# Loading the first token tiles and weights at once, sharing the first squares between two engines, and filling TensorE's first waits with throwaway matmuls

## The chip, the cores and the metric

The kernel runs on all 8 cores of one Trainium2 chip: two dies, cores 0 to 3 and cores 4 to 7. The metric is the device time of the slowest core, in microseconds (us). Every timed run also lists the span and the mean granted TensorE clock of each core. Some runs are in a slow state: one die, or two of its cores, at a lower mean granted clock and behind the others (a run of e5 took 2133 us with die 0 at 0.812 to 0.813 and die 1 at 0.992 to 0.993; one of e1 took 1826 us with cores 6 and 7 at 0.976 to 0.977 and the others at 0.992 to 0.994). They are left out of every comparison here. Three groups of experiments were timed, one on a chip called 2 here and two on a chip called 6; within a group all kernels share the runs of the kernel before.

## The reference, cut to what matters

One step of a decoder layer: a half-step feed-forward block, a mixer (windowed attention, a recurrence, cross attention), a second half-step feed-forward block. Each core takes one prompt of 2048 tokens and 4 sample tokens. Only the start of the first feed-forward block matters here:

```python
D_MODEL = 1024
D_FF = ((8 * D_MODEL // 3 + 127) // 128) * 128   # 2816
EPS = 1e-6

def rmsnorm(x, g):
    xf = x.astype(jnp.float32)
    y = xf * lax.rsqrt(jnp.mean(xf * xf, axis=-1, keepdims=True) + EPS)
    return (y * g.astype(jnp.float32)).astype(x.dtype)

def half_ffn(x, g, w_gate, w_up, w_down):
    h = rmsnorm(x, g)
    return (jax.nn.silu(h @ w_gate) * (h @ w_up)) @ w_down
# ... in reference():
    xp = xp + 0.5 * half_ffn(xp, *ffn1)
# ... mixer, merge, second half_ffn, final rmsnorm
```

## The kernel before

The tokens of a core form six tiles of 336 to 352 tokens. A tile of x lies in SBUF as 128 partitions (features) times 8 chunks of its n tokens, in f32. The head of the kernel is the time until TensorE runs without gaps: tiles 0, 1 and 2 must be loaded, normalised and written as bf16 to `hT` before the gate and up matmuls of the first half can use them. A weight tile (`wp`, from `wgu`) feeds 2 x 8 matmuls for each of the three x tiles, 48 in all.

```python
    def sq(k, c, late=1000.0, pair=True):            # square of chunk c of tile k, summed by TensorE
        n = FT[k][1]
        if c == 0:
            pss[k] = P.tile(psS)
        p = pss[k]
        b = P.tile(brp)
        if not pair:
            actf(b.t[:, 0:n], xv(k, c), AF.Square, [dx[k][c]], [b.d])          # ScalarE
            mm(p.t[:, 0:n], ones_n, b.t[:, 0:n], c == 0, c == 7, [b.d, dc], [p.d], late=late)
        # ... other form, used later

    def lnexp(out, in_, power, reads, writes):       # (mean square + eps) ** power
        actf(out, in_, AF.Ln, list(reads) + [dc], writes, bias=epsc)
        actf(out, out, AF.Exp, writes, writes, scale=power)

    def to_h(k, r, g):                               # VectorE: x * gain * rstd -> hT
        t0, n = FT[k]
        for c in range(8):
            stt(DVE, hT[:, c, t0:t0 + n], xv(k, c), g[:, c:c + 1], r.t[:, 0:n], ALU.mult, ALU.mult, [dx[k][c], r.d, dc], [dh[k][c]])

    def load_x(k, src, parts=1, after=(), queues=(SP,)):
        n = FT[k][1]
        w = 8 // parts
        for q in range(parts):
            dst, sr = xv(k, q * w, w), src[k][:, q * w * n:(q + 1) * w * n]
            P.dma(queues[q % len(queues)], lambda e, dst=dst, sr=sr: e.dma_start(out=dst, in_=sr), reads=list(after), writes=dx[k][q * w:(q + 1) * w])

    def gate_up(half, w, hook=None):
        for j in range(NJ):
            b = load_w(w[j].rearrange("p a c n -> p (a c n)"), 2048, first_w[min(j, 5)] if hook else ())
            wv = b.t[:, :].rearrange("p (a c n) -> p a c n", a=2, c=8)
            for k in HT[half]:
                # ... 8 gate and 8 up matmuls into PSUM, Silu on ScalarE, product on VectorE
            if hook:
                hook(j)

    first_w = [dx[0][0:4], dx[0], dx[1][0:4], dx[1], dx[2][0:4], dx[2]]
# ... the start:
    load_x(0, xt, 4, queues=(SP, ACT))
    # ... constants; vecs (gains) loaded on the ACT queue, behind x
    for k in range(3):
        if k:
            load_x(k, xt, 2, after=dx[k - 1][0:5] if k == 1 else dx[k - 1][0:4])
        for c in range(8):
            sq(k, c, 0.0, False)
        to_h(k, rstd(k), gf1)
```

First, loads are gated: the second tile of x waits for the first, and the j-th weight tile waits for the part of x named in `first_w`. Second, the program is recorded, and a list scheduler in the file decides each engine's order of instructions once, before the run, from believed durations and believed landing times (`DMA_RATE`). On the chip each engine then works in that order, whatever really lands first (the trace below has ScalarE idle for 6.44 us before a square whose data is missing, with an Exp that is ready behind it).

The softmax here doesn't subtract the row's maximum and nothing guards it: scores larger than these inputs give would overflow.

Of the kernel before, what the change touches and what calls it, by code (L numbers as in the profile page):

```python
# [9 lines left out]
ALU = mybir.AluOpType  # L10
# [164 lines left out]
class Prog:  # L175
# [5 lines left out]
    TABLE = 1300.0  # L181
    SWISSUE = 800.0
    WAIT = 1200.0

    def __init__(self, nc, lanes=None):
        self.nc = nc
# [56 lines left out]
    def schedule(self):  # L243
# [61 lines left out]
        while done < n:  # L305
# [76 lines left out]
            if e == ACT and o["aset"] not in (None, table):  # L382
                cost += self.TABLE
                table = o["aset"]
            o["t0"] = start
            if o["dma"]:
                issue = self.SWISSUE if e == POOL else 60.0
                end = free[e] = start + issue
                if o["pool"] == "bulk":
                    fin = start + 12000.0  # L390
                else:
                    pipe[e] = max(pipe[e], start + issue) + o["nbytes"] / self.DMA_RATE[e]
                    fin = pipe[e] + self.DMA_FIX
            else:
                end = free[e] = start + cost
                fin = end + (self.PEDRAIN if e == PE else 0.0)
# [30 lines left out]
    def emit(self):  # L427
        nc = self.nc
        order = self.schedule()
        seq = []  # L430
        pos = {e: 0 for e in COMPUTE}
        for o in sorted(self.all, key=lambda o: o["t0"]):
            e = o["eng"]
            seq.append(order[e][pos[e]])
            pos[e] += 1
        streams, rr = {}, {}
        for o in seq:
            s = o["eng"]
            if o["dma"]:
                q = o["pool"]  # L440
                k = rr.get(q, 0)
                rr[q] = k + 1
                s = ("dma", q, k % self.lanes[q])
            lst = streams.setdefault(s, [])
            o["stream"], o["idx"], o["sig"] = s, len(lst), o["dma"]
            lst.append(o)
        known = {e: {} for e in COMPUTE}
        for o in seq:
            e = o["eng"]
            kn = known[e]  # L450
            deps = {}
            for j in o["preds"]:
                p = self.all[j]
                s, k = p["stream"], p["idx"]
                if not (s == e == PE) and deps.get(s, -1) < k:
                    deps[s] = k
            if o["dma"] and o["idx"] > 0:
                s = o["stream"]
                deps[s] = max(deps.get(s, -1), o["idx"] - 1)
            waits = [(s, k) for s, k in sorted(deps.items(), key=lambda x: str(x[0])) if kn.get(s, -1) < k]  # L460
            o["waits"] = [(s, k) for s, k in waits
                          if not any((s2, k2) != (s, k) and streams[s2][k2]["know"].get(s, -1) >= k for s2, k2 in waits)]
            for s, k in waits:
                for s3, k3 in list(streams[s][k]["know"].items()) + [(s, k)]:
                    if kn.get(s3, -1) < k3:
                        kn[s3] = k3
            for s, k in o["waits"]:
                streams[s][k]["sig"] = True
            o["know"] = dict(kn)
        semval = {}  # L470
        for s, lst in streams.items():
            c, vals = 0, []
            for o in lst:
                if o["sig"]:
                    c += 16 if o["dma"] else 1
                vals.append(c)
            semval[s] = vals
        with ExitStack() as st:
            sems = {}
            for s in streams:  # L480
                if any(o["sig"] for o in streams[s]):
                    sems[s] = st.enter_context(nc.semaphore("s_" + (s if isinstance(s, str) else f"{s[1]}{s[2]}")))
            block = st.enter_context(nc.Block())

            def run(name):
                def body(e):
                    b = Bound(e)
                    for o in order[name]:
                        for s, k in o["waits"]:
                            e.wait_ge(sems[s], semval[s][k])  # L490
                        inst = o["fn"](b)
                        if o["sig"]:
                            inst.then_inc(sems[o["stream"]], 16 if o["dma"] else 1)
                return body
            block.tensor(run(PE))
            block.scalar(run(ACT))
            block.vector(run(DVE))
            block.gpsimd(run(POOL))
            block.sync(run(SP))
# [51 lines left out]
def build_nc():  # L551
    nc = bass.Bass("TRN2", target_bir_lowering=False)
    P = Prog(nc)
# [78 lines left out]
    psS = P.pool(bu[5:8], True, 0)  # L632
    psM = P.pool(bu[0:7], True, 14)
    psO = P.pool(bu[7:8], True, 0)

    ident_f, ones_f = cf[:, 0:128], cf[:, 128:256]
    ident_b, ones_b, ones_n, ones_h = (cb[:, k * 128:(k + 1) * 128] for k in range(4))
# [44 lines left out]
    def load_w(src, n, after=()):  # L682
        b = P.tile(wpool)
        dst = b.t[:, 0:n]
        P.dma(POOL, lambda e: e.dma_start(out=dst, in_=src), reads=list(after), writes=[b.d])
        return b
# [9 lines left out]
    def xv(k, c, m=1):  # L696

        t0, n = FT[k]
        o = 8 * (t0 - 1024 * (k // 3)) + c * n
        return (XA, XB)[k // 3][:, o:o + m * n]  # L700
# [4 lines left out]
    def sq(k, c, late=1000.0, pair=True):  # L705
# [12 lines left out]
        else:  # L718
# [2 lines left out]
            tt(POOL, b.t[:, 0:n], s.t[:, 0:n], s2.t[:, 0:n], ALU.add, [s.d, s2.d], [b.d])  # L721
            mm(p.t[:, 0:n], ones_n, b.t[:, 0:n], c == 1, c == 7, [b.d, dc], [p.d], late=late)

    def rstd(k):
        n = FT[k][1]
        r = P.tile(frp)
        p = pss[k]
        lnexp(r.t[:, 0:n], p.t[:, 0:n], -0.5, [p.d], [r.d])
        return r
# [13 lines left out]

    def gate_up(half, w, hook=None):
        for j in range(NJ):
            b = load_w(w[j].rearrange("p a c n -> p (a c n)"), 2048, first_w[min(j, 5)] if hook else ())
            wv = b.t[:, :].rearrange("p (a c n) -> p a c n", a=2, c=8)
            for k in HT[half]:
                t0, n = FT[k]
                pg, pu = P.tile(psA), P.tile(psA)  # L750
                for p, a in ((pg, 0), (pu, 1)):
                    for c in range(8):
                        mm(p.t[:, 0:n], wv[:, a, c, :], hT[:, c, t0:t0 + n], c == 0, c == 7, [b.d, dh[k][c]], [p.d])
                s = P.tile(frp)
                actf(s.t[:, 0:n], pg.t[:, 0:n], AF.Silu, [pg.d], [s.d])
                o = t0 - 1024 * half
                tt(DVE, act[:, j, o:o + n], pu.t[:, 0:n], s.t[:, 0:n], ALU.mult, [pu.d, s.d], [dact[half][k % 3]])
            if hook:
                hook(j)

    first_w = [dx[0][0:4], dx[0], dx[1][0:4], dx[1], dx[2][0:4], dx[2]]

    def down(half, w, done):
        def one(k, dp, bs):
# [594 lines left out]
        return 1760e3  # L1359


    load_x(0, xt, 4, queues=(SP, ACT))
    P.op(POOL, lambda e: e.memset(vec[:, 60:61], 1.0), writes=[d_one])
    P.op(ACT, lambda e: e.activation(out=vec[:, 63:64], in_=vec[:, 60:61], func=AF.Ln), reads=[d_one], writes=[d_one])
    P.op(DVE, lambda e: e.memset(ones_n, 1.0 / 1024), writes=[dc])
    P.op(DVE, lambda e: e.memset(vec[:, 61:62], EPS), writes=[dc])
    P.op(DVE, lambda e: e.memset(vec[:, 62:63], 0.0), writes=[dc])
    P.dma(ACT, lambda e: e.dma_start(out=vec[:, 0:52], in_=vecs), writes=[dc])
    for k in range(3):
        if k:  # L1370
            load_x(k, xt, 2, after=dx[k - 1][0:5] if k == 1 else dx[k - 1][0:4])
        for c in range(8):
            sq(k, c, 0.0, False)
        to_h(k, rstd(k), gf1)
    P.op(POOL, lambda e: e.memset(ones_b, 1.0), writes=[dm])
    P.op(POOL, lambda e: e.memset(ones_h, 1.0 / 128), writes=[dm])
    P.op(POOL, lambda e: e.memset(rst, 1.0), writes=[dm])
    P.op(POOL, lambda e: e.memset(cb[:, 896:1408:64], 0.0), writes=[dm])
    for q, (src_, dst_) in enumerate(bulk):
        dd = Dep()  # L1380
        P.dma(ACT, lambda e, src_=src_, dst_=dst_: e.dma_start(out=dst_, in_=src_), writes=[dd], pool="bulk", rel=bulk_at(q / nbulk))
# [1 line left out]
    def hook(j):  # L1383
        if j == 3:
            mem_load()
        elif j == 5:
            P.dma(ACT, lambda e: e.dma_start(out=cf[:, :], in_=cstf), reads=d_memT, writes=[dm])
            P.dma(POOL, lambda e: e.dma_start(out=cb[:, 0:128], in_=cstb[:, 0:128]), reads=d_memT, writes=[dm])
            P.dma(POOL, lambda e: e.dma_start(out=cb[:, 512:896], in_=cstb[:, 128:512]), writes=[dm])
        elif j == 6:  # L1390
            mem_norm()
        elif j in (7, 8):
            mem_k(j - 7)
        elif j == 9:
            mem_v()
        elif j in (10, 12, 14):
            k = 3 + (j - 10) // 2
            switch(dx[k], d_memT + d_mhT)
            load_x(k, xt)
        elif j in (16, 18, 20):  # L1400
            k = 3 + (j - 16) // 2
            for c in range(8):
                sq(k, c)
            to_h(k, rstd(k), gf1)
# [222 lines left out]
```

## Time and profile before

| | before |
|---|---|
| time, median of 3 runs | 1809.42 us (1807.29 to 1811.98) |
| spans of the cores in the profiled run | 1797.5 to 1802.6 us |
| core 2 (slowest), `hT` of tiles 0, 1, 2 begun | 22.3, 31.8, 42.9 us |
| core 2, 97th gate/up matmul (the third weight tile) begun | 53.5 us |

The profiled run is not itself one of the timed runs, so its spans are compared only with spans. A count is taken from the trace, in which a matmul may be missing now and then (the page below lists 12105 matmuls and 12171 weight loads).

The first part of the page of the kernel before (core 2) gives busy time, share of the span and number of instructions by engine:

```profile
PE 1738.2 (96%) x12105; PEld 1109.0 (62%) x12171; DVE 674.7 (37%) x1391; ACT 730.4 (41%) x1266; POOL 405.2 (22%) x543
```

TensorE (PE) is the limit, at 96%. What can be won lies where it isn't busy, and that is the head. Stretches of 10 us of core 2; the columns are from:to, length, busy us with instruction counts of each engine, the granted TensorE clock (1.00 is full), the DMA engines' busy share and GB/s:

```profile
core 2: us, PE busy (x) PEld busy (x) DVE busy (x) ACT busy (x) POOL busy (x), PEclk, DMA share, GB/s
20.00:30.00 10.00, 5.30 (x24) 2.77 (x24) 4.58 (x9) 7.35 (x12) 1.59 (x3) 1.00 0.99 263
30.00:40.00 10.00, 7.80 (x40) 4.47 (x40) 3.95 (x9) 6.95 (x14) 1.06 (x2) 0.83 1.04 196
40.00:50.00 10.00, 6.42 (x26) 3.48 (x27) 4.86 (x10) 5.94 (x12) 0.00 (x0) 0.66 0.64 143
```

In a full stretch later on, TensorE does about 70 matmuls in 10 us (73 from 80 to 90 us, at a granted clock of 1.00); here it does 24, 40 and 26, and part of them at a granted clock of 0.66 to 0.83. The timeline of core 2 shows the chain (start, duration, engine, operation, output and inputs, count; in brackets the idle time before it and what ended it). In these lines `XA` is x, `br` a square, `hb` the sum of squares in PSUM, `fr` what ScalarE writes (Ln, Exp or Silu), `ps` and `nd` the gate and up results in PSUM, `wp` a weight tile:

```profile
14.17 0.56 ACT L80 ACTIVATE fr<-hb,vec 128x352 f32<-128x352 f32 x1 [0.69 <-PE hb L80]
21.17 0.57 ACT L80 ACTIVATE br<-XA,vec 128x336 bf16<-128x336 f32 x1 [6.44 <-DMA XA<-xt]
21.65 0.57 ACT L80 ACTIVATE fr<-fr,vec 128x352 f32<-128x352 f32 x1
22.32 4.06 DVE L80 SCALAR_TENSOR_TENSOR hT<-XA,vec,fr 128x352 bf16<-128x352 f32 x8 [20.59 <-ACT fr L80]
...
31.78 3.92 DVE L80 SCALAR_TENSOR_TENSOR hT<-XA,vec,fr 128x336 bf16<-128x336 f32 x8 [2.18 <-ACT fr L80]
...
42.87 3.92 DVE L80 SCALAR_TENSOR_TENSOR hT<-XA,vec,fr 128x336 bf16<-128x336 f32 x8 [1.93 <-ACT fr L80]
```

Read the first three lines together: ScalarE takes the Ln of tile 0 at 14.17, then waits 6.44 us for a part of x tile 1 to square it, because that square comes next in its order, and only then does the Exp of tile 0. The normalisation of tile 0 (22.32) is late because of the order, not because of its own data. The waits of TensorE on core 2 up to 60 us (total, times, longest) say the same from the other end:

```profile
PE hb L80 <- ACT br L80: 22.9, 5, 10.3
PE ps L80 <- DVE hT L80: 3.8, 1, 3.8
```

It waits 22.9 us for squares (`br`) and 3.8 us for `hT`. Finally the DMA view of core 2, window 12 to 32 us, by queue (q0 is the GpSimd queue of the weights, q1 the SyncE queue of x, and q10 the ScalarE queue):

```profile
q0 software_dynamic: 477, 1.76, 54.3%
q1 hardware_dynamic: 576, 2.75, 46.2%
```

In these 20 us x tiles 1 and 2 came in whole: 4 loads of 128 rows. The last figure is the share of the 16 DMA engines' time. The spans of this run:

```profile
core 0: 1798.7 us, clock 0.993
core 1: 1802.2 us, clock 0.993
core 2: 1802.6 us, clock 0.993
core 3: 1798.6 us, clock 0.993
...
die 0 (median of its cores): 1800.4 us, clock 0.993
die 1 (median of its cores): 1800.0 us, clock 0.993
```

### The profile page before, as it was taken

To read this page: it belongs to the slowest core of one execution; us is meant where nothing else is said; L and a number is where in the kernel's file an instruction comes from. 1 tells how busy PE (TensorE), PEld (TensorE's weight loads), DVE (VectorE), ACT (ScalarE), POOL (GpSimd) and SP (SyncE) were. 2 spreads that over 40 slices of the span, in tenths; PEclk is the share of its full clock that TensorE was granted. 3 is DMA by queue.
4 is the path that set the end of the run, shared out by engine and by line. 5 is a ranking of instruction groups with operands and counts; after the bars stand their busy time and mean duration, and the time that the engine had idled before them with its cause. 6 is when DMAs were issued, how large, how long until landed. Compare 5 with 4: busy or idle time off the path is not lost.

```text
span 1802.6 us, 33178 instructions; the slowest of 8 cores (1797.5 to 1802.6 us)
## 1 busy us (share of the span) xinstructions
PE 1738.2 (96%) x12105; PEld 1109.0 (62%) x12171; DVE 674.7 (37%) x1391; ACT 730.4 (41%) x1266; POOL 405.2 (22%) x543
## 2 busy tenths in 40 slices
PE   4999999999999999999999999999999999999996
PEld 1666666666655545555556566666666666666663
DVE  2223314222142435756576533543452221422213
ACT  5334414222145566758776633433342221322212
POOL 1112221001244051433431122322220002100021
PEclk9999999999999999999999999999999999999998
DMA  8486459656688554654547745596875447899562
GB/s 196 80 167 127 70 102 197 123 122 127 120 211 199 142 120 77 122 98 93 96 100 152 170 80 88 106 193 130 164 147 87 69 104 145 163 192 171 104 141 96
DMA packets 89391, 234.00 MB, mean 130 GB/s; under 512 B 32912, under 2 KB 40336, under 8 KB 86416
## 3 DMA queue, kind: packets, MB, share of 16 engines
q0 software_dynamic: 40608, 127.03, 44.6%
q1 hardware_dynamic: 46224, 59.26, 10.4%
q10 hardware_dynamic: 2400, 45.57, 8.7%
q8 instruction: 102, 1.67, 0.4%
q14 instruction: 57, 0.47, 0.1%
HBM read 321.27 MB, written 80.51 MB: 223 GB/s over the span
## 4 chain that ended last, share of the span: by engine, by line
PE 90%; DVE 3%; ACT 3%; issue 2%; DMA 1%; POOL 1%; DVEq 0%; ACTq 0%; SPq 0%; POOLq 0%
PE ps L80 49%; PE nd L80 33%; PE hb L80 8%; DVE XB L80 1%; ACT fr L80 1%; DMA XA<-xt 1%; DVE hT L80 1%; DVE br L80 1%; ACT br L80 0%; ACT L80 0%; ACT XA L80 0%; DVE fr L80 0%; POOL XA L80 0%; DVE XA L80 0%; POOL fr L80 0%
## 5 line engine op out<-in xcount | busy, mean ns | idle before, releaser
L80 PE MATMUL ps<-hT,wp 128*128 128x336 bf16 (+4 forms) x3839 | 637.2, 312 | 5.7 <-DVE hT L80 3.8
L80 PEld LDWEIGHTS ps<-hT,wp 128*128 128x128 bf16 x3856 | 365.6, 98 | 208.3 <-issue 6.4
L80 PE MATMUL nd<-hT,wp 128*128 128x336 bf16 (+4 forms) x2547 | 434.5, 312 | 1.4 <-ACT fr L80 0.2
L80 PEld LDWEIGHTS nd<-hT,wp 128*128 128x128 bf16 x2560 | 243.3, 98 | 134.7 <-issue 2.0
L80 ACT ACTIVATE fr<-ps,vec 128x336 f32<-128x336 f32 (+3 forms) x269 | 150.1, 560 | 343.8 <-PE ps L80 343.4
L80 PE MATMUL ps<-actb,wp 128*128 128x336 bf16 (+2 forms) x1612 | 253.8, 308 | 0.3 <-DVE XB L80 0.3
L80 PEld LDWEIGHTS ps<-actb,wp 128*128 128x128 bf16 x1612 | 157.3, 98 | 76.7 <-issue 0.6
L80 ACT ACTIVATE fr<-nd,vec 128x336 f32<-128x336 f32 (+3 forms) x185 | 103.4, 560 | 235.5 <-PE nd L80 235.2
L80 DVE TENSOR_TENSOR actb<-ps,fr 128x336 bf16<-128x336 f32 (+2 forms) x160 | 81.9, 514 | 266.2 <-PE ps L80 260.9
L80 PE MATMUL nd<-actb,wp 128*128 128x336 bf16 (+2 forms) x1076 | 173.0, 308 | 0.7 <-ACT fr L80 0.7
L80 POOL TENSOR_TENSOR fr<-fr 128x512 f32<-128x512 f32 (+3 forms) x96 | 108.0, 1132 | 161.0 <-DVE fr L80 140.2
L80 POOL DMA_DIRECT2D wp<-wgu x88 | 47.4, 538 | 400.3 <-PE ps L80 229.9
L80 PEld LDWEIGHTS nd<-actb,wp 128*128 128x128 bf16 x1076 | 105.0, 98 | 52.3 <-issue 1.0
L80 POOL TENSOR_TENSOR br<-fr 128x336 bf16<-128x336 f32 (+2 forms) x84 | 77.3, 923 | 181.2 <-ACT fr L80 181.0
L80 DVE TENSOR_TENSOR actb<-nd,fr 128x336 bf16<-128x336 f32 (+2 forms) x104 | 53.2, 513 | 173.2 <-PE nd L80 167.2
L80 ACT ACTIVATE fr<-XB,vec 128x352 f32<-128x352 f32 (+2 forms) x96 | 53.9, 577 | 138.5 <-DVE XB L80 138.5
L80 PE MATMUL hb<-hT,wp 128*128 128x512 bf16 (+1 forms) x514 | 95.2, 312 | 1.0 <-ACT fr L80 0.2
L80 ACT ACTIVATE fr<-XA,vec 128x336 f32<-128x336 f32 (+1 forms) x72 | 40.9, 578 | 130.2 <-DVE XA L80 130.2
L80 POOL DMA_DIRECT2D wp<-wd x64 | 34.8, 544 | 249.6 <-PE ps L80 128.5
L80 PE MATMUL hb<-br,cb 128*128 128x336 bf16 (+7 forms) x188 | 48.5, 300 | 28.9 <-ACT br L80 22.9
L80 ACT ACTIVATE fr<-fr,vec 128x512 f32<-128x512 f32 (+3 forms) x105 | 72.6, 700 | 5.0
L80 DVE SCALAR_TENSOR_TENSOR fr<-fr,ps 128x336 f32<-128x336 f32 (+2 forms) x85 | 43.2, 510 | 77.6 <-ACT fr L80 77.6
(244 smaller groups left out, 1630.9 us busy)
## 6 DMA issues: line engine op xcount, KB each, us to landing
wp<-wgu POOLq DMA_DIRECT2D x88, 512.0 KB, 8.9
wp<-wd POOLq DMA_DIRECT2D x64, 352.0 KB, 5.8
wp<-w_gb POOLq DMA_DIRECT2D x48, 384.0 KB, 8.8
wp<-w_hqf POOLq DMA_DIRECT2D x16, 512.0 KB, 8.3
vd<-br SPq DMA_DIRECT2D x48, 128.0 KB, 4.0
XA<-vd SPq DMA_DIRECT2D x12, 512.0 KB, 5.7
wp<-w_qk POOLq DMA_DIRECT2D x12, 512.0 KB, 7.6
pv<-fr SPq DMA_DIRECT2D x21, 256.0 KB, 6.4
```

The lines of the kernel that those rows point to most:

```text
L80: return f(*[g(x) for x in a], **{n: g(x) for n, x in k.items()})
```

## The change

The intent is to start everything at once and to use the engines that stand idle in the head. The gains (`vecs`) are loaded first. All three x tiles are loaded in four parts each, on the SyncE and ScalarE queues in turn, without gates; the weights lose their gates too, so three queues work from the start. The squares may go to ScalarE or VectorE, whichever the scheduler thinks will be done first. In TensorE's waits during the first 60 us, as the scheduler foresees them, throwaway matmuls are put in, to keep the granted clock up (before, on core 2, it was 0.50 from 44 to 48 us, right after a wait of 3.8 us). One memset moves from GpSimd to VectorE, and four on GpSimd are recorded later.

```diff
@@ class Prog
+    HEAD = 20000.0
+    HEAD_RATE = 105.0
+    fill, fill_end, FILL = None, 0.0, 80.0
@@ schedule
+            if e == PE and order[PE] and self.fill is not None and start < self.fill_end:
+                o["fill"] = max(0, int((start - free[e] - 150.0) / self.FILL))
...
-                    pipe[e] = max(pipe[e], start + issue) + o["nbytes"] / self.DMA_RATE[e]
+                    t = max(pipe[e], start + issue)
+                    pipe[e] = t + o["nbytes"] / (self.HEAD_RATE if t < self.HEAD else self.DMA_RATE[e])
@@ emit
+                        for _ in range(o.get("fill", 0)):
+                            self.fill(e)
@@ squares of the first three tiles
+    def sq_first(k, c):
+        # ... PSUM tile from a pool of two banks
+        P.op((ACT, DVE), (lambda e: e.activation(out=b.t[:, 0:n], in_=x, func=AF.Square, bias=zeroc, scale=1.0),
+                          lambda e: e.tensor_tensor(out=b.t[:, 0:n], in0=x, in1=x, op=ALU.mult)), reads=[dx[k][c], dc], writes=[b.d])
+        mm(p.t[:, 0:n], ones_n, b.t[:, 0:n], c == 0, c == 7, [b.d, dc], [p.d])
@@ gate_up
-            b = load_w(w[j].rearrange("p a c n -> p (a c n)"), 2048, first_w[min(j, 5)] if hook else ())
+            b = load_w(w[j].rearrange("p a c n -> p (a c n)"), 2048)
...
-    first_w = [dx[0][0:4], dx[0], dx[1][0:4], dx[1], dx[2][0:4], dx[2]]
@@ start
-    load_x(0, xt, 4, queues=(SP, ACT))
+    P.dma(ACT, lambda e: e.dma_start(out=vec[:, 0:52], in_=vecs), writes=[dc])
+    for k in range(3):
+        load_x(k, xt, 4, queues=(SP, ACT))
...
-    P.dma(ACT, lambda e: e.dma_start(out=vec[:, 0:52], in_=vecs), writes=[dc])
+    P.op(PE, lambda e: e.matmul(bu[7].t[:, 0:128], lhsT=ones_n, rhs=ones_n, start=True, stop=True), reads=[dc])
+    P.fill = lambda e: e.matmul(bu[7].t[:, 0:128], lhsT=ones_n, rhs=ones_n, start=True, stop=True)
+    P.fill_end = 60e3
     for k in range(3):
-        if k:
-            load_x(k, xt, 2, after=dx[k - 1][0:5] if k == 1 else dx[k - 1][0:4])
         for c in range(8):
-            sq(k, c, 0.0, False)
+            sq_first(k, c)
         to_h(k, rstd(k), gf1)
-    # ... four memsets on POOL, moved into the hook at j == 5
```

Nothing after the head is changed in the source; the later parts of the schedule may still shift.

More of the change, by code (lines that the diff above doesn't have):

```diff
@@ L634, in build_nc @@
     psO = P.pool(bu[7:8], True, 0)
+    psS0 = P.pool(bu[5:7], True, 0)
     ident_f, ones_f = cf[:, 0:128], cf[:, 128:256]
@@ L722, in sq @@
             mm(p.t[:, 0:n], ones_n, b.t[:, 0:n], c == 1, c == 7, [b.d, dc], [p.d], late=late)
+    def sq_first(k, c):
+        n = FT[k][1]
+        if c == 0:
+            pss[k] = P.tile(psS0)
+        p, b, x = pss[k], P.tile(brp), xv(k, c)
+        P.op((ACT, DVE), (lambda e: e.activation(out=b.t[:, 0:n], in_=x, func=AF.Square, bias=zeroc, scale=1.0),
+                          lambda e: e.tensor_tensor(out=b.t[:, 0:n], in0=x, in1=x, op=ALU.mult)), reads=[dx[k][c], dc], writes=[b.d])
+        mm(p.t[:, 0:n], ones_n, b.t[:, 0:n], c == 0, c == 7, [b.d, dc], [p.d])
     def rstd(k):
@@ L1359, in bulk_at @@
         return 1760e3
-    load_x(0, xt, 4, queues=(SP, ACT))
-    P.op(POOL, lambda e: e.memset(vec[:, 60:61], 1.0), writes=[d_one])
+    P.dma(ACT, lambda e: e.dma_start(out=vec[:, 0:52], in_=vecs), writes=[dc])
+    for k in range(3):
+        load_x(k, xt, 4, queues=(SP, ACT))
+    P.op(DVE, lambda e: e.memset(vec[:, 60:61], 1.0), writes=[d_one])
     P.op(ACT, lambda e: e.activation(out=vec[:, 63:64], in_=vec[:, 60:61], func=AF.Ln), reads=[d_one], writes=[d_one])
@@ L1367, in build_nc @@
     P.op(DVE, lambda e: e.memset(vec[:, 62:63], 0.0), writes=[dc])
-    P.dma(ACT, lambda e: e.dma_start(out=vec[:, 0:52], in_=vecs), writes=[dc])
+    P.op(PE, lambda e: e.matmul(bu[7].t[:, 0:128], lhsT=ones_n, rhs=ones_n, start=True, stop=True), reads=[dc])
+    P.fill = lambda e: e.matmul(bu[7].t[:, 0:128], lhsT=ones_n, rhs=ones_n, start=True, stop=True)
+    P.fill_end = 60e3
     for k in range(3):
-        if k:
-            load_x(k, xt, 2, after=dx[k - 1][0:5] if k == 1 else dx[k - 1][0:4])
         for c in range(8):
-            sq(k, c, 0.0, False)
+            sq_first(k, c)
         to_h(k, rstd(k), gf1)
-    P.op(POOL, lambda e: e.memset(ones_b, 1.0), writes=[dm])
-    P.op(POOL, lambda e: e.memset(ones_h, 1.0 / 128), writes=[dm])
-    P.op(POOL, lambda e: e.memset(rst, 1.0), writes=[dm])
-    P.op(POOL, lambda e: e.memset(cb[:, 896:1408:64], 0.0), writes=[dm])
     for q, (src_, dst_) in enumerate(bulk):
@@ L1386, in hook @@
         elif j == 5:
+            P.op(POOL, lambda e: e.memset(ones_b, 1.0), writes=[dm])
+            P.op(POOL, lambda e: e.memset(ones_h, 1.0 / 128), writes=[dm])
+            P.op(POOL, lambda e: e.memset(rst, 1.0), writes=[dm])
+            P.op(POOL, lambda e: e.memset(cb[:, 896:1408:64], 0.0), writes=[dm])
             P.dma(ACT, lambda e: e.dma_start(out=cf[:, :], in_=cstf), reads=d_memT, writes=[dm])
```

## The prediction

> **What bounds it now.** TensorE: 1738 of 1802.6 us busy (page, part 1); the table of stretches has it 99.9% busy from 50 to 400 us; the waits add 14 us in the middle, the tail some 10. The exception is the head: by 51.2 us TensorE has done 89 gate/up matmuls and 24 sums of squares, at the warm pace of 0.143 us (timeline after 50 us) about 16 us of work. About 35 us are lost there; the change can't win more.
>
> **The head's chain (before, core 2).** x tile 0 lands at 9.0 us; its squares wait until 9.5 for the gains (vecs), queued behind x. Its normalisation's Exp then sits behind an x1 square in ScalarE's order until x1's first half lands (21.1). First gate/up matmul: 23.1. Tile 1 is squared by 26.0, but ScalarE does Silu first, with two table loads of 1.28 us: hT of tile 1 at 31.8. x2 lands about 32.1; squares, Silu, two more table loads: hT of tile 2 at 42.9, TensorE flows from 43.6, cold (0.28 us per matmul) until 49.3, which costs about 2.9 us. DMA is 0.86 to 1.06 busy from 10 to 45 us: the loads share a saturated resource.
>
> **What the change does.** x1 and x2 (2.7 MB) and seven weight tiles (0.5 MB each as stored) no longer wait for earlier loads. This adds no bandwidth. [...]the trace agrees (x1 12 to 14 us beside weights, x0 7 us alone). Estimate: from 10.3 to 32 us about 4.8 MB landed, 220 GB/s. One x queue beside one weight queue got about half; two should get two thirds, 145 to 175 GB/s. Then x0 lands at 11 to 13 us (later than now), x1 at 19 to 22, x2 at 26 to 31. Vecs come first.
> Squares take 0.56 us each; on two engines the last quarter needs about 0.6. x landing to hT should be 3 to 5 us including a table load, not 10.7. PSUM rings let TensorE run only one group ahead of a missing tile, so the gain is set by hT of tile 2: 42.9 becomes 31 to 36, 7 to 12 us. The throwaway matmuls keep the clock up ([...]the slow matmuls after each wait agree) and save 1 to 3 us, most at tile 2. The moved memsets are off the path.
>
> **Prediction.** 1797 us, about 12 us (0.7%) less; 8 in 10: 1789 to 1805. Faster by over 2%: 0.02; within 2%: 0.97; slower: 0.01.
>
> **What would show it.** First real matmul at 14 to 17 us, not 23; hT of tile 2 at 31 to 36; TensorE gapless from there; DMA near 1.0 from 2 to 35 us without the gap at 9 to 10; gate/up soon at 0.14 us; stretches after 60 us unchanged but shifted.
>
> **What would make it wrong.** Weights crowd out x more (x2 at 36: gain 5), or less (x2 at 23: gain 18). The scheduler believes in x arriving earlier than it does, and fixes in-order queues: a late tile's square ahead of a ready normalisation on VectorE would block it. Fill matmuls longer than the real wait delay real work. A shifted schedule in the mixer: a few us either way.

The forecast's sum is 7 to 12 us from tile 2 and 1 to 3 us from the clock, 8 to 15 us together, of which the prediction took 12. That the throwaway matmuls keep the clock up is the estimate from the slow matmuls (0.28 us against 0.143) after the waits.

## The result, and the profile after

| | before | after |
|---|---|---|
| time, median of 4 runs each | 1809.26 us (1807.29 to 1811.98) | 1804.02 us (1802.20 to 1804.88) |
| die 0, median span in the profiled run | 1800.4 us | 1796.2 us |
| core 2, `hT` of tiles 0, 1, 2 begun | 22.3, 31.8, 42.9 us | 17.8, 35.9, 39.7 us |
| all cores, `hT` of tile 2 begun | 38.1 to 44.3 us | 39.7 to 40.8 us |
| core 2, 97th gate/up matmul begun | 53.5 us | 48.2 us |
| all cores, 97th gate/up matmul begun | 48.6 to 53.5 us | 48.2 to 50.8 us |

The ratio of the times is 0.9969, with a 95% interval of 0.9951 to 0.9986. Ratios throughout are the mean time of one kernel's fast runs over that of the other's in the same rounds, so they are not quite the ratios of the medians quoted. The gain is 5.2 us; 12 us were forecast. It lies within the range, and it is less than half of the forecast. The new row on all cores tells why core 2 alone can mislead: on cores 0, 3, 4 and 6 tile 2 was normalised at 38.1 to 40.8 us before, so for these the change moved it by under 2 us, on two of them later and on two earlier. What gained there is the slow core of each pair (1, 2, 5 and 7, 42.5 to 44.3 us before).

The slowest core of the profile after is core 5 (1802.3 us, TensorE at 97%). To compare like with like, the lines below are of core 2 again. Its stretches:

```profile
20.00:30.00 10.00, 4.52 (x26) 1.84 (x25) 4.60 (x10) 3.92 (x6) 0.00 (x0) 0.92 1.01 229
30.00:40.00 10.00, 8.12 (x62) 5.95 (x63) 5.05 (x11) 5.71 (x10) 0.00 (x0) 0.74 1.02 198
40.00:50.00 10.00, 10.00 (x71) 6.65 (x70) 6.00 (x13) 7.11 (x15) 1.59 (x3) 1.00 0.56 148
```

The stretch from 40 to 50 us is now full (71 matmuls, clock 1.00, against 26 at 0.66). The two before it are not: at 20 to 30 us TensorE is as poor as it was (and its matmuls now include throwaway ones), and the DMA engines' busy share stands at 1.01 to 1.02, with no idle time left. The timeline of core 2 has the chain:

```profile
17.83 4.06 DVE L80 SCALAR_TENSOR_TENSOR hT<-XA,vec,fr 128x352 bf16<-128x352 f32 x8 [2.60 <-ACT fr L80]
...
25.85 1.04 ACT L80 ACTIVATE br<-XA,vec 128x336 bf16<-128x336 f32 x2 [4.72 <-DMA XA<-xt]
...
30.89 1.04 ACT L80 ACTIVATE br<-XA,vec 128x336 bf16<-128x336 f32 x2 [2.13 <-DMA XA<-xt]
31.94 1.28 ACT L80 ACT_TABLE_LOAD   x1
33.24 0.54 ACT L80 ACTIVATE fr<-hb,vec 128x336 f32<-128x336 f32 x1
34.73 0.58 ACT L80 ACTIVATE br<-XA,vec 128x336 bf16<-128x336 f32 x1 [0.95 <-DMA XA<-xt]
35.21 0.56 ACT L80 ACTIVATE fr<-fr,vec 128x336 f32<-128x336 f32 x1
...
35.87 7.76 DVE L80 SCALAR_TENSOR_TENSOR hT<-XA,vec,fr 128x336 bf16<-128x336 f32 x16 [4.22 <-ACT fr L80]
```

Tile 0 is normalised 4.5 us earlier than before. The last part of tile 1 lands at 25.8 and is squared at once, but its Ln and Exp stand behind squares of tile 2 on ScalarE, which wait for their data until 30.89 and 34.73: tile 1 is normalised at 35.87, later than before (31.78). It is the pattern of the kernel before, one tile further on. Tile 2 lands complete at 34.6 and follows straight after tile 1 (the group of 16 is both tiles; the second begins at 39.7). Its own Exp was done at 38.0 on ScalarE, so the last 1.7 us of it are VectorE still busy with the late tile 1. Each of the two table loads of ScalarE between 25 and 35 us took 1.28 us; the one at 31.94 began as the square before it ended (31.93), and the Ln followed at 33.24. TensorE's waits on core 2 up to 60 us:

```profile
PE hb L80 <- ACT br L80: 9.9, 6, 3.8
PE hb L80 <- DVE vec L80: 5.4, 1, 5.4
PE ps L80 <- DVE hT L80: 0.5, 1, 0.5
```

The waits for squares fell from 22.9 to 9.9 us, partly because throwaway matmuls now fill them; the 5.4 us are the wait for the constants at the very start. The DMA view of core 2, window 15 to 25 us, in which all three queues have work all the time:

```profile
q0 software_dynamic: 269, 0.97, 57.5%
q1 hardware_dynamic: 273, 0.65, 23.7%
q10 hardware_dynamic: 272, 0.65, 19.8%
```

The three queues moved 269, 273 and 272 packets: in this window they took equal turns, and a packet is one row (the counts can't tell one row per turn from a few rows per turn; the shares are the same). But a row of x is now a quarter tile wide (2 chunks of 336 f32, 2688 bytes) where it was half a tile (5376 bytes), and a weight row is 4096 bytes as written. So two x queues get 2 x 2688 of 9472 bytes per round, 57%, and measured the same 57% (1.30 of 2.28 MB) and 130 GB/s (1.30 MB in 10 us). One x queue with rows twice as long had 5376 of 9472, the same 57%, and measured 138 GB/s (61%; its window includes a time, 21.3 to 22.8 us, in which the gated weights moved nothing). The change doubled the x queues and halved their rows, and the share did not grow. In engine time the weights cost even more than their 43% of the bytes: 57.5% in the lines above.

A second thing delayed x, and the prediction chose it: "Vecs come first". The issues of the first 5 us on core 2, with the median time from issue to landing in the last column:

```profile
XA<-xt SPq DMA_DIRECT2D x4, 336.0 KB, 20.0
XA<-xt ACTq DMA_DIRECT2D x4, 336.0 KB, 25.1
```

Loads issued at nearly the same time land 5 us later on the ScalarE queue, which has the gains in front. On all cores the SyncE queue landed its last part of x at 30.0 to 31.2 us, at the upper end of the forecast's 26 to 31, and the ScalarE queue landed its last part, which completes x2, at 34.6 to 35.7 us, 3.6 to 5.4 us after it: it runs one load behind throughout. How much earlier x2 would be complete with the gains elsewhere was not tested beside ungated weights (e12 moves them, but only behind x0 and with the weights held back); as an estimate these 3.6 to 5.4 us are the most that it could be.

The total throughput hardly moved: 228 GB/s in this window (2.28 MB in 10 us), against 226 GB/s before from 12 to 32 us (4.51 MB in 20 us).

The spans:

```profile
core 0: 1796.3 us, clock 0.994
core 1: 1795.9 us, clock 0.993
core 2: 1796.1 us, clock 0.994
core 3: 1796.4 us, clock 0.992
...
die 0 (median of its cores): 1796.2 us, clock 0.994
die 1 (median of its cores): 1801.8 us, clock 0.989
```

Two things are new here. Before, in this profile, cores 1 and 2 were 3.5 to 4 us slower than cores 0 and 3; that unevenness is gone on die 0. And die 1 is 5.6 us slower than die 0, at a lower granted clock: its trace has 5 to 7 dips of the granted clock to 0.8125, each 4 to 6 us long, spread over the whole run (at 533, 656, 676, 1018 and 1554 us on core 5). On cores 6 and 7 there are two more, at 44.9 and 1325 us, which cores 4 and 5 don't have. All four timed runs of the changed kernel show die 1 at a clock of 0.987 to 0.992. Since the metric is the slowest core, the time is that of die 1.

From the 97th matmul to the end, core 2 took 1749.1 us before (1802.6 - 53.5) and 1747.9 us after (1796.1 - 48.2). On a die without dips, about 1 us of the gain comes after the head and all else from within it.

### The profile page after: what moved, and what is told of

The parts are those of the page before. It is cut to its first block, busy times and chain, and to the rows that moved or that the text cites. A ratio compares the mean times of both kernels' runs of the same rounds, so it can differ in the third digit from the quotient of the medians.

```text
span 1802.3 us, 33516 instructions; the slowest of 8 cores (1795.9 to 1802.3 us)
## 1 busy us (share of the span) xinstructions
PE 1755.1 (97%) x12305; PEld 1120.6 (62%) x12305; DVE 682.0 (38%) x1404; ACT 724.2 (40%) x1252; POOL 403.2 (22%) x542
## 3 DMA queue, kind: packets, MB, share of 16 engines
q1 hardware_dynamic: 46224, 57.89, 10.1%
## 4 chain that ended last, share of the span: by engine, by line
PE 92%; DVE 2%; DMA 2%; ACT 2%; issue 1%; POOL 0%; ACTq 0%; DVEq 0%; POOLq 0%
PE ps L80 50%; PE nd L80 34%; PE hb L80 8%; DMA XA<-xt 2%; DVE XB L80 1%; ACT fr L80 1%; DVE br L80 1%; DVE hT L80 0%; ACT br L80 0%; ACT XA L80 0%; ACT L80 0%; DVE fr L80 0%; POOL XA L80 0%; ACTq L80 0%; DVE XA L80 0%
## 5 line engine op out<-in xcount | busy, mean ns | idle before, releaser
L80 PE MATMUL ps<-hT,wp 128*128 128x336 bf16 (+4 forms) x3928 | 651.5, 312 | 0.6 <-ACT fr L80 0.3
L80 PEld LDWEIGHTS ps<-hT,wp 128*128 128x128 bf16 x3928 | 371.4, 98 | 207.4 <-issue 3.6
L80 ACT ACTIVATE fr<-ps,vec 128x352 f32<-128x352 f32 (+3 forms) x276 | 154.4, 561 | 350.5 <-PE ps L80 350.0
L80 PE MATMUL hb<-hT,wp 128*128 128x512 bf16 (+1 forms) x400 | 75.2, 320 | 0.0
L80 DVE SCALAR_TENSOR_TENSOR fr<-fr,ps 128x336 f32<-128x336 f32 (+2 forms) x86 | 43.6, 510 | 78.3 <-ACT fr L80 74.6
L80 PE MATMUL hb<-br,cb 128*128 128x336 bf16 (+6 forms) x200 | 47.8, 290 | 16.3 <-ACT br L80 10.4
```

The lines of the kernel that those rows point to most:

```text
L80: return f(*[g(x) for x in a], **{n: g(x) for n, x in k.items()})
```

## The experiments

Twelve runs, in three groups of four. All gave correct results. "Before" in each group means the kernel before, timed in the same rounds. "#97" stands for the start of the 97th gate/up matmul, the measure of the head; ranges are over the cores.

The theory: x is still too slow, because queues take turns by rows and the ungated weights take 43% of the bytes; with x2 at 35 us, nothing downstream can help. The rivals: the order on ScalarE (wrong belief about landing times) is what holds the head; or the fills delay real work; or the gain is made and lost later, to the clock.

### e1_after_again: the changed kernel, on chip 2

No edit.

> The changed kernel once more, as the reference of this group. In the first profile the gain in the head was small: counted on all cores, the 97th gate/up matmul started at 48.2 to 50.8 us, against 48.6 to 53.5 before. x2 landed at 34.6 to 35.7. Theory (gain lost in the head): the ratio to before is again 0.995 to 0.999, and the 97th gate/up matmul comes at 48 to 51. Rival (most of the gain was there and was eaten by the dips of the granted clock to 0.8125, five to seven of 4 to 5 us each, that only die 1 showed): if this chip shows no dips in this kernel, the ratio falls to 0.994 or below; if dips come back on the same die, they are of the kernel and not of the chip.

Ratio to before 0.9952 (0.9935 to 0.9970), with only 2 of 6 runs fast: 1798.51 and 1798.86 us against a mean of 1807.47 for before. Three runs near 1826 us had two cores of one die, 6 and 7, some 28 us behind the others; in the one with a trace they ran at 0.8125 for 160 us, from 43 us on (mean clocks over the run 0.976 and 0.977, against 0.992 to 0.994 on the other cores). One run took 2020 us. In the two fast runs all cores span 1796 to 1797 us, and their mean clocks, 0.992 to 0.994, leave no sign of dips. The ratio is the theory's (0.995 to 0.999), not the rival's 0.994 or below, though the interval doesn't exclude it. So on this chip, in the fast state, the same kernel wins 8.8 us: before's slowest core of each die lay at 1805.7 and 1804.8 us (means), the changed kernel's at 1797. The head's landings and #97 (48.2 to 48.7 us on cores at full clock) are those of the run after.

### e2_longer_rows: rows of x tiles 1 and 2 twice as long

```diff
-        load_x(k, xt, 4, queues=(SP, ACT))
+        load_x(k, xt, 2 if k else 4, queues=(SP, ACT))
```

> Only x1 and x2 are cut in two loads of 5.4 KB rows instead of four of 2.7 KB rows. Theory (the engines serve the three queues row by row in turn, so a queue's share goes with its row length): while one weight tile of 128 rows lands, so do 128 rows of each x queue, 1.9 MB at 233 GB/s, 8.1 us: x1 lands at 22 to 24 us instead of 25.7, x2 at 30 to 32 instead of 34.6, the second weight tile at 22 to 24 instead of 19.5. Rival (queues share by bytes): x1 stays at 25 to 26 and x2 at 34 to 35. The order of the in-order queues changes too, so the time is not for this alone; if both act, the 97th gate/up matmul starts at 43 to 46 us and the ratio to before is about 0.994.

The DMA view of core 2, window 16 to 23 us:

```profile
q0 software_dynamic: 146, 0.53, 47.1%
q10 hardware_dynamic: 146, 0.70, 31.4%
q1 hardware_dynamic: 112, 0.52, 22.0%
```

The weights and one x queue moved 146 packets each, the other x queue 112, and x now has 1.22 of 1.75 MB, 70%, or 174 GB/s (1.22 MB in 7 us); equal turns would give 72%. x1 landed at 23.1 to 24.4, as expected, and x2 at 27.7 to 29.1 us, 6 to 7 us earlier than in the changed kernel and 1 to 4 earlier than the 30 to 32 expected. The rival, x2 at 34 to 35 with shares that don't depend on rows, is refuted. Nothing else about the loads was touched, so it is shown that the share went with row length here: 57% for x with rows of 2688 bytes, 70% with 5376.

The head did not follow: `hT` of tile 2 began at 38.9 to 41.8 us and #97 at 46.7 to 49.3, not at the 43 to 46 expected. Tile 2's squares stood behind tile 1's normalisation on VectorE, and Silu stood with its table loads between Ln and Exp on ScalarE. The scheduler still believed in the old landing times. The mean time was 1799.49 us, ratio to before 0.9956 (0.9943 to 0.9970), the same as e1.

### e3_true_rates: the scheduler is told the measured rates

No load is issued otherwise; only the belief changes, and with it each engine's order.

```diff
-    HEAD = 20000.0
-    HEAD_RATE = 105.0
+    HEAD = 36000.0
+    HEAD_RATE = {SP: 66.0, ACT: 66.0, POOL: 200.0}
-        pipe, table = {e: 0.0 for e in COMPUTE}, None
+        pipe, table = {e: 6000.0 * (e == POOL) for e in COMPUTE}, None
```

> Only the scheduler's belief about the head's loads changes: 66 GB/s for each x queue and 200 (as read) for the weight queue until 36 us, first weights 6 us late, as measured. No load is issued otherwise. Theory (the order fixed on wrong arrival times put the Exp of tile 1 on ScalarE behind a square of tile 2 and so held back tile 1's hT by 7 us): landings stay (x2 34 to 36), hT of tile 1 starts at 29 to 31 instead of 36, the 97th gate/up matmul at 44 to 46 instead of 48.2 to 50.8, 3 to 4 us faster than the changed kernel. Rival (the loads alone set the head, the order is hidden behind them): 97th gate/up matmul at 48 to 50, time within 1 us of the changed kernel.

Landings were unchanged. `hT` of tile 1 began at 29.5 to 30.1 us instead of 36, as expected: the square of tile 2 no longer stood before tile 1's Exp. Yet #97 moved by only 1.3 us, to 47.0 to 47.7 (44 to 46 was expected), because `hT` of tile 2 stayed at 39.5 to 40.1. So the wrong order on ScalarE is real and costs 6 us on tile 1, but is worth at most 1.3 us in the head; the landing of x2 limits. Even the 1.3 us are not the order's alone: the fills follow the same belief. With the measured rates the scheduler put in 257 of them instead of 133, and the granted clock stayed at 1.00 from 10 to 50 us on all cores, where e1 shows 0.64 to 0.78 from 30 to 40 us. The ratio, 0.9984 (0.9940 to 1.0028), says little: the fast runs include one of 1824 us and one of 1804 us. The three clean ones took 1797.43, 1797.75 and 1798.66 us, within about 1 us of e1's two, as the rival said.

### e4_no_fill: the changed kernel without throwaway matmuls

```diff
-    P.fill_end = 60e3
+    P.fill_end = 0.0
```

> The changed kernel without throwaway matmuls (one stays); the order of everything else is the same. Theory: in the changed kernel the clock still fell to half between 28 and 38 us, when it was needed, because the fills run before each wait in a number fixed by the scheduler and end long before the loads come; so they are worth little: the 97th gate/up matmul comes 0 to 2 us later, time plus 0 to 2 us. Rival (the fills carry the gain): plus 3 us or more, gate/up matmuls at 0.28 us for 6 us more.

Mean 1801.57 us (5 of 5 fast), ratio to before 0.9968 (0.9956 to 0.9980), so 2.9 us slower than e1's two fast runs; #97 at 49.6 to 50.6 us, 1.6 us later; some 20 to 30 gate/up matmuls at the slow pace, against 0 to 8. The fills are worth 1.6 to 2.9 us, where 0 to 2 were expected. That they delay real work is refuted in sum: without them landings and `hT` of tile 2 (39.5 to 40.6 us) stay, and #97 and the end come later.

### e5_gated_weights: the changed kernel with the weights' gates of before

```diff
-            b = load_w(w[j].rearrange("p a c n -> p (a c n)"), 2048)
+            b = load_w(w[j].rearrange("p a c n -> p (a c n)"), 2048, first_w[min(j, 5)] if hook else ())
...
+    first_w = [dx[0][0:4], dx[0], dx[1][0:4], dx[1], dx[2][0:4], dx[2]]
```

> The changed kernel with one part undone: the first weight tiles wait for the x parts again, as in the kernel before; all x loads still go out at once. Theory (weights issued at once crowd x out row for row): each weight tile is held back by about one round, so x2 lands at 28 to 31 us instead of 34.6 to 35.7 and the 97th gate/up matmul starts at 43 to 47 us instead of 48.2 to 50.8; 2 to 5 us faster than the changed kernel. Rival (the weights were needed early and gating them costs as much): x2 earlier, but the first gate/up matmul later than 18.3 and the 97th no earlier than 48. The cores should stay within 1 us of each other if it is the loads of x going out at once that makes them equal; if they spread by 3 to 5 us as in the kernel before, it was the gating of the weights that spread them.

x0 was complete at 11 us, x1 at 15.9 to 18.1, x2 at 26.1 to 28.0 (28 to 31 was expected). `hT` of tile 2 began at 31.9 to 33.9 us, which is the forecast's 31 to 36, and #97 at 43.0 to 44.4, as expected. The first weight tile landed only at 20.3 to 21.8, so the first gate/up matmul started at 20.4 to 21.9, about 2 us later than in the changed kernel, and the head was shorter all the same: TensorE had to wait for tile 2 in any case. Ratio to before 0.9942 (0.9923 to 0.9961), 5 of 6 fast. The expectation's question on the cores is answered too: in the fast runs those of die 0 spread by 2.0 to 3.5 us again, so the gates on the weights have a part in the unevenness of the kernel before. The direct comparison with the changed kernel on the same chip is e9 and e10 below.

### e6_halves_rates and e8_halves_rates_no_fill: all x in longer rows, and the belief adjusted; without and with fills removed

```diff
-    HEAD = 20000.0
-    HEAD_RATE = 105.0
+    HEAD = 26000.0
+    HEAD_RATE = {SP: 88.0, ACT: 88.0, POOL: 131.0}
-        load_x(k, xt, 4, queues=(SP, ACT))
+        load_x(k, xt, 2, queues=(SP, ACT))
# e8 also: P.fill_end = 0.0
```

> All three x tiles in two loads each, one per queue, rows of 5.4 to 5.6 KB, so that a round of 128 rows per queue carries a whole x tile and one weight tile; the scheduler's rates set to that (88 GB/s per x queue, 131 for weights as read, until 26 us). Theory (row-by-row turns, and the right order on the in-order engines): x0 and the first weight tile land at 10 to 11.5 us, x1 and the second at 18 to 20, x2 at 26 to 28; hT of tile 0 at 13 to 15, tile 1 at 22 to 24, tile 2 at 30 to 33; the 97th gate/up matmul at 38 to 42 us; 6 to 10 us faster than the changed kernel, ratio to before 0.989 to 0.992. Rival (order or rows alone can't be had together, another wait takes over): 97th at 45 or later.

x2 landed at 27.4 to 30.0 us, as expected, but `hT` of tile 2 began at 37.8 to 40.0 and #97 at 46.1 to 48.4 us; the 30 to 33 and 38 to 42 of the theory were missed and the rival came true. The timeline of core 2 shows the new wait:

```profile
27.50 0.33 SPq L80 DMA_DIRECT2D XB<-memt  x1
28.73 3.92 DVE L80 SCALAR_TENSOR_TENSOR hT<-XA,vec,fr 128x336 bf16<-128x336 f32 x8 [2.33 <-ACT fr L80]
32.57 1.75 DVE L80 TENSOR_TENSOR br<-XA 128x336 bf16<-128x336 f32 x4
38.22 3.92 DVE L80 SCALAR_TENSOR_TENSOR hT<-XA,vec,fr 128x336 bf16<-128x336 f32 x8 [2.61 <-ACT fr L80]
```

The first line is issued when x2 has landed. VectorE then normalises tile 1 (28.73) before it squares its part of tile 2 (32.57), so 5 us pass between the landing of x2 and those squares. x0 was late too, at 14.6 to 16.6 instead of 10 to 11.5, with the 128 short rows of the gains ahead of it on the ScalarE queue (e12 tests this: with them behind x0 it landed 3 to 4 us earlier). Ratio to before 0.9975 (0.9953 to 0.9997), mean 1806.96 us.

> The previous candidate without throwaway matmuls. Theory: 97th gate/up matmul 1 to 3 us later than with them (cold start at the first real matmul and after the wait for tile 2), time plus 1 to 3 us. And on the long dips of the granted clock to 0.8125 that begin at 43 us on two cores of one die: they came in 3 of 6 and 2 of 6 runs of two kernels with fills and in 0 of 5 of the one without; if fills provoke them, this one has none again and the one with fills has some; if both have some, fills are not the cause.

Ratio 0.9971 (0.9951 to 0.9991), mean 1806.24 us (4 of 7 fast). #97 came at 49.0 to 51.5, about 3.3 us later than in e6, with some 30 to 50 slow matmuls against 2 at most, yet the time was no worse. Die 0's median was 3.8 us longer than e6's (1799.1 against 1795.3, over the fast runs), as the head says; it was die 1 that evened the times out. Short dips to 0.8125 are there without fills too (in e8's trace at 537 us; the mean clocks of die 1 in that run were 0.991 to 0.992, those of die 0 0.993 to 0.994), so the fills alone don't cause those. The long dips from 43 us on, which the expectation asked about, show in no run of e5 to e8, with fills or without (none has two cores alone some 28 us behind), so their cause stays open.

### e7_act_squares: the changed kernel with all first squares on ScalarE

```diff
-        P.op((ACT, DVE), (lambda e: e.activation(out=b.t[:, 0:n], in_=x, func=AF.Square, bias=zeroc, scale=1.0),
-                          lambda e: e.tensor_tensor(out=b.t[:, 0:n], in0=x, in1=x, op=ALU.mult)), reads=[dx[k][c], dc], writes=[b.d])
+        P.op(ACT, lambda e: e.activation(out=b.t[:, 0:n], in_=x, func=AF.Square, bias=zeroc, scale=1.0), reads=[dx[k][c], dc], writes=[b.d])
```

> The changed kernel with one part undone: all first squares on ScalarE. Theory (the loads set the head; the squares of a tile come one by one with its parts, and only the last two are on the chain): the 97th gate/up matmul within 2 us of the changed kernel's 48.2 to 50.8, time within 2 us. Rival (sharing the squares is what gained): 4 us or more later.

#97 came at 50.6 to 52.4 us, some 2.3 us later than in the changed kernel, and the cores of die 0 took 1799.7 us on average, 3.1 us over the 1796.6 of the changed kernel in the third group on the same chip (the kernel before was itself 0.9 us slower on die 0 in e7's group). Ratio to before 0.9989 (0.9959 to 1.0019). About 2 us of it is a wait near 49 us that comes from the new order itself (squares of a later tile placed ahead of a Silu), so what the sharing alone is worth stays open between nothing and 3 us.

### e9_after_beside and e10_gated_beside: the changed kernel and the gated one on the same chip

e9 is the changed kernel, e10 is the kernel of e5.

> The changed kernel, to stand on the same chip beside the gated one. Expected as before: 97th gate/up matmul at 48.2 to 50.8 us; ratio to before 0.995 to 0.997.

> The gated weights once more, beside the changed kernel on one chip. Theory (letting the first weights out at once is the part of the change that costs): 97th gate/up matmul at 43 to 45 us, 3 to 5 us faster than the changed kernel in fast runs of the same chip, also in the spans of a die whose clock doesn't dip. Rival: the earlier group's difference was of the chip; within 1.5 us.

| mean of the fast runs | before | e9, the change | e10, weights gated | e11, see below |
|---|---|---|---|---|
| time | 1809.05 | 1804.81 | 1801.82 | 1798.96 |
| ratio to before (95%) | | 0.9976 (0.9963 to 0.9988) | 0.9959 (0.9947 to 0.9972) | 0.9943 (0.9931 to 0.9956) |
| slowest core of die 0 | 1803.6 | 1797.0 | 1793.8 | 1792.6 |
| slowest core of die 1 | 1807.5 | 1803.2 | 1800.3 | 1797.3 |

The head of e10: x2 at 25.0 to 28.4 us, `hT` of tile 2 at 31.1 to 34.6, #97 at 41.4 to 44.7, against 48.3 to 49.2 in e9. One line of its timeline on core 0, the normalisation of tile 2, shows what the change as made doesn't reach:

```profile
32.57 3.92 DVE L80 SCALAR_TENSOR_TENSOR hT<-XA,vec,fr 128x336 bf16<-128x336 f32 x8 [2.49 <-ACT fr L80]
```

With the gates back, the cores of die 0 are on average 4.0 us faster than with the change as made (1792.6 against 1796.6), and the kernel 3.0 us. So of the parts of the change, "weights at once" costs about 4 us and everything else together wins more than the change's total. Against e9 tile 2 was normalised 7.5 us earlier and #97 began 5.6 us earlier (means).

### e11_late_gates: first weight tile free, the others gated later, and the belief to match

```diff
-    HEAD = 20000.0
-    HEAD_RATE = 105.0
+    HEAD = 26000.0
+    HEAD_RATE = {SP: 92.0, ACT: 92.0, POOL: 200.0}
-        pipe, table = {e: 0.0 for e in COMPUTE}, None
+        pipe, table = {e: 6000.0 * (e == POOL) for e in COMPUTE}, None
-            b = load_w(w[j].rearrange("p a c n -> p (a c n)"), 2048)
+            b = load_w(w[j].rearrange("p a c n -> p (a c n)"), 2048, first_w[min(j, 5)] if hook else ())
+    first_w = [(), dx[1][0:4], dx[2][0:4], dx[2], dx[2], dx[2]]
```

> A candidate: the first weight tile goes out at once, the second after the first half of x1, the third after the first half of x2, the rest after x2; all x at once in four parts; scheduler's rates 92 GB/s per x queue and 200 for weights as read, first weights 6 us late, until 26 us. Theory (bytes ahead of x2 set hT of tile 2, and the order follows the arrivals): x0 and first weights at 14 to 15, x1 at 19.5 to 22, x2 at 24.5 to 27; hT of tile 2 at 29 to 32; 97th gate/up matmul at 40 to 43; 1 to 4 us faster than the gated kernel of this group. Rival (VectorE and ScalarE now set the head): hT of tile 2 at 33 or later although x2 has landed by 27, no faster than the gated kernel.

The best version: 1798.96 us (5 of 5 fast, 1798.59 to 1799.49), 10.1 us under before and 5.9 us under the changed kernel (ratio to it 0.9968). x2 landed at 21.7 to 23.7 us, the earliest of all, but `hT` of tile 2 began at 36.1 to 36.9 and #97 at 43.6 to 44.5, no earlier than in e10; 29 to 32 and 40 to 43 were expected, so on the head the rival was right. The timeline of core 1:

```profile
22.80 0.33 SPq L80 DMA_DIRECT2D XB<-memt  x1
...
27.25 3.92 DVE L80 SCALAR_TENSOR_TENSOR hT<-XA,vec,fr 128x336 bf16<-128x336 f32 x8 [1.44 <-ACT fr L80]
31.10 0.92 DVE L80 TENSOR_TENSOR br<-XA 128x336 bf16<-128x336 f32 x2
...
36.07 3.92 DVE L80 SCALAR_TENSOR_TENSOR hT<-XA,vec,fr 128x336 bf16<-128x336 f32 x8 [1.61 <-ACT fr L80]
```

x2 is there at 22.8, and its normalisation begins at 36.07, 13 us later: the DMA no longer limits the head, VectorE's and ScalarE's orders do. Against e10 the time is 2.9 us shorter, but die 0's slowest core only 1.2 us; the time is set by die 1, where dips come and go (its mean clocks are 0.992 to 0.994 in e11's fast runs and 0.990 to 0.994 in e10's, those of die 0 0.993 to 0.997), so the rest can't be credited to the edit.

### e12_late_gates_vecs: e11 with the gains loaded behind x0

```diff
-    P.dma(ACT, lambda e: e.dma_start(out=vec[:, 0:52], in_=vecs), writes=[dc])
...
     for k in range(3):
         load_x(k, xt, 4, queues=(SP, ACT))
+        if k == 0:
+            P.dma(ACT, lambda e: e.dma_start(out=vec[:, 0:52], in_=vecs), writes=[dc])
# the memsets and squares wait for constants of their own (dz), not for the gains
```

> The same, with the small gains load behind x0 on its queue instead of ahead of it, and the squares waiting for the memsets alone. Theory (in turns by row, the 128 short rows of the gains cost the ScalarE queue as many turns as an x part, so x0 lands a round late): x0 complete at 10 to 12 us instead of 14.5, hT of tile 0 at 14 to 16 instead of 17.7; x2 unchanged within 1 us, so 97th gate/up matmul within 1 us and time within 1.5 us of the candidate without it. Rival (the gains load costs by its bytes, 26 KB, nothing): x0 stays at 14 to 15.

x0 was complete at 10.7 to 12.6 us (e11: 14.7 to 15.5), as the theory expected, while the gains' 26 KB, now behind x0, took until 14.6 to 15.9, and #97 came at 42.3 to 43.5, about 1 us earlier. The time was 1800.76 us (5 of 8 fast), ratio to before 0.9955 (0.9941 to 0.9969): no better than e11, with die 0 equal within 0.4 us. Landing x0 3 to 4 us earlier bought about 1 us at #97 and nothing that could be measured in the time.

## Why the prediction was right or wrong

**Wrong: the gain, 5.2 us for 12.** The mechanism was right and a size was off. The step that failed, in the prediction's words: "One x queue beside one weight queue got about half; two should get two thirds, 145 to 175 GB/s", from which "x2 at 26 to 31" and "42.9 becomes 31 to 36". Measured: 57% and 130 GB/s, x2 complete at 34.6 to 35.7, `hT` of tile 2 at 39.7 to 40.8. On core 2 that term was forecast at 7 to 12 us and came to 3.2. The reasoning counted queues and took each as an equal share. The queues did get equal turns (269, 273 and 272 packets), but the bytes of a turn went with the row (0.97, 0.65 and 0.65 MB), and the same diff that added a queue halved the rows. The "about half" was the share of engine time (46%); by bytes x already had 61%. It could have been worked out from the trace before, where 477 packets of one queue carried 1.76 MB and 576 of the other 2.75 MB. Two experiments confirm the term from two sides: with rows twice as long x gets 70% (e2), and with fewer weights beside it `hT` of tile 2 begins at 31.1 to 34.6 us (e5, e10), where the forecast had it. The part of the miss that belongs to "Vecs come first", at most 3.6 to 5.4 us of x2's landing, is read from the trace and not tested. The prediction did list the outcome ("Weights crowd out x more (x2 at 36: gain 5)"), but not as its centre.

**Right: no bandwidth is added.** The total stayed at 226 to 228 GB/s between before and after. "This adds no bandwidth" held. (In e2's window the total was higher, 1.75 MB in 7 us or 250 GB/s, so it is not the same for every mix of rows; why was not tested.)

**Right: tile 2 sets the head.** "The gain is set by hT of tile 2" held: repairing tile 1 by 6 us moved #97 by 1.3 us (e3), while repairing tile 2 by gating the weights moved it by about 5.6 us (e9 to e10).

**Half right: "x landing to hT should be 3 to 5 us".** For tile 2 it about held (34.6 to 39.7 on core 2, 1.7 us of it behind tile 1). For tile 1 it took 10 us (25.8 to 35.9). The prediction named this hazard, a static order fixed on too early landing times, but placed it on VectorE; in the changed kernel it sat on ScalarE. In e2, e6 and e11 it did appear on VectorE, as soon as the loads were faster.

**Wrong, and without cost: the first gate/up matmul** at 18.3 to 19.9 us, not 14 to 17. x0 was complete at 14.5 to 15.1 instead of 11 to 13 (the gains' short rows were ahead of it; with them behind it in e12 it was complete at 10.7 to 12.6). In e5 it came 2 us later still, and the head was shorter; that the delay cost nothing is inferred from this, not measured by itself.

**Right: the fills**, "1 to 3 us": 1.6 to 2.9 us (e4), and 3.3 us at #97 in e6 against e8. Before, the granted clock was 0.50 on core 2 from 44 to 48 us, after TensorE had waited 3.8 us for `hT` of tile 2, and some 35 to 40 gate/up matmuls took about 0.28 us, against 0 to 19 after (0.14 to 0.15 us at full clock). From 30 to 40 us the granted clock of core 2 was 0.53 without the fills (e4) and 0.74 with them. The fills were cut to the believed waits, which are shorter than the real ones: the 0.74 is still below the 0.83 of before. In e3, where the belief fits and 257 fills stand instead of 133, it stays at 1.00 from 10 to 50 us.

**Not foreseen: what the metric does with the cores.** The slowest core of each die gained more than the median: 6.6 us on die 0 in the third group (1803.6 to 1797.0), because in the kernel before one core of each pair (0 and 1, 2 and 3, and so on) was 2 to 7 us behind the other in each of these runs, and after the change those of die 0 are level. Against that, die 1 lost time at a lower granted clock on chip 6 in both kernels (in the third group its mean clocks were 0.989 to 0.993 before and 0.986 to 0.991 after, those of die 0 0.991 to 0.994): it was 3.9 us behind die 0 before (1807.5 against 1803.6) and 6.2 us after (1803.2 against 1797.0). On chip 2, in the two fast runs, the mean clocks show no sign of dips and the gain was 8.8 us. So, as an estimate, of the missing 7 us some 4 belong to the share of the DMA (what e10 wins back on die 0) and some 2 to the clock of die 1 in these runs (6.2 less 3.9). Whether the change provokes more dips, and whether it makes the slow state more frequent, stays open: the kernel before has the slow state too (4 of 37 runs, against 6 of 17 of the changed kernel), and the runs are too few to tell.

**Open:** what the sharing of the squares is worth by itself (e7), what issuing the gains elsewhere would win, and why one core of each pair was slower before. Of the last the record shows a part. In the trace before, the spread is there when the first half of x1 lands: 14.8 to 17.6 us on cores 0, 3, 4 and 6, 20.3 to 21.1 on the others. And with the weights gated again the cores of die 0 spread by 1.9 to 3.5 us (fast runs of e5 and e10), against 0.3 to 1.7 in e9.

## What to carry to other kernels

When loads compete, count bytes per turn and not queues. In this kernel a queue's share went with the length of its rows (x got 57% with rows of 2688 bytes on two queues, 70% with 5376), so cutting x into narrower parts gave bandwidth to the weights beside it, and what brought the critical load in earliest was to hold back the others until it had landed (x2 at 21.7 to 23.7 us in e11 and 25.0 to 28.4 in e10, against 34.6 to 35.7). A load that is made faster pays only up to the next wait (in e11 x2 was there at 22.8 us on core 1 and was normalised at 36.07), and on engines with a fixed order that wait was often an instruction for another tile; tell the scheduler the landing times that the trace shows. A small load of many short rows in front of a critical one wasn't free either: x0 landed 3 to 4 us later behind the 128 rows of the gains (e11 against e12). Read the gain on each die before believing the time of the slowest core.
